# A fourth buffer for streamed weights in a two-block transformer kernel

## The chip, the core and the metric

The kernel is one program on one core of a Trainium2 chip, started once. What is compared is the device time of one execution in microseconds (us); of several executions the median counts. The engines are TensorE (PE; PEld is its weight load, which overlaps the multiplication), VectorE (DVE), ScalarE (ACT), GpSimd (POOL) and SyncE (SP), which here only issues DMAs. They run side by side and wait for each other by semaphores.

## The reference, cut to what matters

256 tokens of width 1024 pass through two different blocks. Each of the two layers of the first block multiplies by `w_in`, mixes in three ways and multiplies by `w_out`:

```
h = x @ w_in[l]                       # 1024 x 6048, split into ten parts
y_hg  = hgrn2(q, f, i)                # chunked gated recurrence, 8 heads
y_mla = mla(cq, ckv, kr)              # attention over latents, 8 heads
y_mem = attention(mem_q, mem @ w_mem_k, mem @ w_mem_v)
x = layernorm(ALPHA * x + concat(y * silu(gates)) @ w_out[l])
```

The second block modulates by `w_ada` (one row of 6144 numbers from `silu(c)`), attends with dilated windows, pools over four trailing windows, and looks up experts:

```
mod  = silu(c) @ w_ada + b_ada                      # 1024 x 6144
q, k, v, u = split(modulated_rmsnorm(x) @ w_in)
x = x + g1 * (concat(dilated_attention(q, k, v), pool(u)) @ w_out)
h2 = modulated_rmsnorm(x)
eid, gate = top 16 of 128 x 128 product keys, 8 heads per token
x = x + g2 * sum_k gate_k * gelu(h2 . expert_u[eid_k]) * expert_v[eid_k]
out = rmsnorm(x)
```

Everything is float32. A product is made of three TensorE products: `a = ah + al`, where `ah` is `a` rounded to the engine's fast 32-bit form, and `ah*bh + ah*bl + al*bh` is accumulated.

## The kernel before, in words

**The stream of weights.** Every large weight comes through one path. `load` (L168) takes a 512 KB tile named `raw` (128 partitions x 1024 numbers) from the pool `wp` and has SP issue the DMA (L170). `split` (L158) lets ACT copy it to `wh` (L162) and DVE subtract to `wl` (L163). `wp` has three buffers of each of the three names. A `raw` buffer is free when its last reader, the subtraction on DVE, is done; a `wh` and a `wl` when the matmuls that read them are (`mm3`, L216 to L218). `feature` uses two such units of 1024 columns for a bank of 256-column products, `token` four for two banks of 512-column products.

**The stream of modulation weights.** `w_ada` goes through the same `raw` buffers (48 loads), but is read by DVE alone, which adds it, scaled by a number for each partition, to `macc` (L892, L894). A generator `ada_parts` yields between the loads; `tick`, which is called after each unit of weights, advances it at every third unit in the layers and at every unit in the second block. There weights and modulation rows so take turns in the ring of three. Larger tiles (`ws`, `wo`, `wq`, constants) have their own buffers, and SP issues them in the same queue.

**Side work.** Attention and recurrence are generators too, resumed by `tick` between two units, so their small instructions stand between the products on every engine. Each engine executes its instructions in the order that the tile scheduler wrote down when the program was built; the scheduler orders by its own estimates of when operands and buffers are ready, so the number of buffers and their sharing reach into the order of every engine.

**Buffers in the order of the program.** `mla_qkv` (L480) writes the normalized latents `cn` in the pool `ml`; the memory queries `mq` (L676) are in the same pool. `xn`, the normalized input of the second block (L724), shares one slot of the pool `xnp` with the keys `kt` of the layers. `yph` and `ypl` (L1015) are the pooled features, in the pool `bp`.

**Warm matmuls.** `warm` (L220) issues matmuls that nobody reads, on a tile of zeros, behind the last real one: 27 at the start, 50 between the blocks (while x is normalized for the second block), 13 before the experts.

**The experts.** POOL issues 256 indirect gathers of 1 MB (L1254); their first needs the experts' indices of the first token tile, which come from a chain through the whole of both blocks. DVE and PE consume the rows (L1320, L1332).

Of the kernel before, what the change touches and what calls it, by code (L numbers as in the profile page):

```python
# [8 lines left out]
F = mybir.dt.float32  # L9
R = mybir.dt.float32r  # L10
# [8 lines left out]
S = 256  # L19
# [12 lines left out]
WARM = (27, 50, 13)  # L32
# [116 lines left out]
class Prog:  # L149
# [16 lines left out]
        return wh, wl  # L166

    def load(self, src, n):  # L168
        raw = self.wp.tile([128, 1024], F, name="raw")
        self.nc.sync.dma_start(raw[:, :n], src)  # L170
        return raw

# [44 lines left out]
        mm(ps, a[0], b[1], start=False, stop=False)  # L217
        self.last_mm = mm(ps, a[1], b[0], start=False, stop=stop)  # L218

    def warm(self, n, ps=None):  # L220

        if ps is None:
            ps = self.pph.tile([128, 512], F, name="bank")
        for _ in range(n):
            m = self.nc.tensor.matmul(ps, self.zero, self.zero[:, None, :].to_broadcast([128, 4, 128]), start=True, stop=True)
            if self.last_mm is not None:
                self.tc.add_manual_dep(m.ins, self.last_mm.ins.name, NOSYNC, reason="fills the time behind it")

# [251 lines left out]
    def mla_qkv(self, l, pm, rows, ws, out):  # L480

        nc = self.nc
        cn = self.ml.tile([128, 2, 416], F, name="cn")
        ss = self.sm.tile([128, 4], F, name="ss")
        sq = self.h2.tile([128, 384], F, name="pt", bufs=2)
        for tt in range(2):
            nc.scalar.activation(sq[:, :256], pm[tt][:, :256], AF.Square, accum_out=ss[:, tt:tt + 1])
            nc.scalar.activation(sq[:, 256:], pm[tt][:, 256:384], AF.Square, accum_out=ss[:, 2 + tt:3 + tt])
        self.rstd(ss[:, 0:2], ss[:, 0:2], 1.0 / 256, self.eps6)
        self.rstd(ss[:, 2:4], ss[:, 2:4], 1.0 / 128, self.eps6)  # L490
        for tt in range(2):
            nc.vector.scalar_tensor_tensor(cn[:, tt, :256], pm[tt][:, :256], ss[:, tt:tt + 1], rows[:, 128:384], op0=OP.mult, op1=OP.mult)
            nc.scalar.activation(cn[:, tt, 384:], pm[tt][:, 384:416], AF.Copy)
            nc.vector.scalar_tensor_tensor(cn[:, tt, 256:384], pm[tt][:, 256:384], ss[:, 2 + tt:3 + tt], rows[:, 384:512], op0=OP.mult, op1=OP.mult)
        return self.mla_rest(ws, cn, out)
# [122 lines left out]
    def layer(self, l, x, xt, mem):  # L618
        nc, I = self.nc, self.I
# [10 lines left out]
        n = 4  # L630
# [45 lines left out]
        mq = self.ml.tile([128, 4, S], F, name="mq")  # L676
        for j in range(2):
            ps = self.feature(W[n], xt)
# [15 lines left out]
        def halves(cg):  # L694
            nonlocal n
            n += 1
            for j, u in enumerate(self.half_units(W[n - 1])):
                yield j, [t.rearrange("p (k c) -> p k c", k=2) for t in u]
# [21 lines left out]
        us = list(halves(1))  # L720
# [7 lines left out]
        for tt in range(2):  # L728
# [8 lines left out]
            for cg in range(2):  # L737
                c = slice(cg * 512, (cg + 1) * 512)
# [7 lines left out]
            if l + 1 == NL:  # L746
                self.normed(x, tt, ss[tt], self.xn[:, tt, :])
        if l + 1 == NL:
            self.warm(WARM[1])
            return None, None  # L750
        xt = self.affine_transposed(x, self.lnc[:, l, 0, :], self.lnc[:, l, 1, :], lambda kg: self.new_xt(), self.h2, "pt")
        mv = self.mem_values(l + 1, nxt[1])
# [220 lines left out]
    def block2(self, x, bp, bk, hp, wq):  # L973

        nc, I = self.nc, self.I
        W, xn = I["wu2"], self.xn
# [6 lines left out]
        wp = bp.tile([128, 512], F, name="wpool")  # L983
# [15 lines left out]
        def tokens(t, j):  # L999
            ps = self.token([W[j], W[j + 1]], ht)  # L1000
            for tt in range(2):
                nc.scalar.activation(t[:, tt, :], ps[tt], AF.Copy)
# [3 lines left out]
        for h in range(8):  # L1006
            for tt in range(2):
                c = slice(128, 384) if tt else slice(0, 128)
# [3 lines left out]
        features(1)  # L1012
        self.start(self.dilated((4, 5), 0, qT, kT, v, y))
        tokens(u, 6)
        yp = [bp.tile([128, 4, S], R, name=n) for n in ("yph", "ypl")]  # L1015
        self.pooling(u, band, wp, yp, bp)
        self.pph.release()
        self.pacc.release()
# [32 lines left out]
        def hidden(tt, ss):  # L1051

            t = bk.tile([128, D], F, name="xn")
            self.normed(x, tt, ss, t)
            yield
            for j in range(2):
                ps = self.pps.tile([128, 4, 128], F, name="bank")
                for k in range(4):
                    f = 4 * j + k
                    nc.tensor.transpose(ps[:, k, :], t[:, f * 128:(f + 1) * 128], self.ident)  # L1060
                for k in range(4):
                    f = 4 * j + k
                    d = self.hidden[:, f, tt * 128:(tt + 1) * 128]
                    scale, shift = self.mod[4][:, f:f + 1], self.mod[3][:, f:f + 1]
                    if k % 2:
                        nc.vector.tensor_scalar(d, ps[:, k, :], scale, shift, op0=OP.mult, op1=OP.add)
                    else:
                        nc.scalar.activation(d, ps[:, k, :], AF.Identity, scale=scale, bias=shift)
                yield
# [20 lines left out]
        for _ in attended(0):  # L1090
            pass
        self.hid = self.big.tile([128, D], F, name="big")
        self.warm(WARM[2], self.hid[:, 0:512])
        for _ in hidden(0, ss[0]):
            pass

# [243 lines left out]
def body(tc, I, O):  # L1340
    nc = tc.nc
    p = Prog(tc, I)
    with tc.tile_pool(name="c0", bufs=1) as c0, tc.tile_pool(name="xp", bufs=1) as xp, tc.tile_pool(name="sm", bufs=4) as sm, \
            tc.tile_pool(name="mo", bufs=1) as mo:
        p.pps, p.pacc, p.pph = [tc.alloc_tile_pool(name=n, bufs=b, space=PSUM) for n, b in (("pps", 2), ("pacc", 4), ("pph", 2))]
        x = xp.tile([128, 2, D], F, name="x")
        wp = tc.alloc_tile_pool(name="wp", bufs=3)
        xnp = tc.alloc_tile_pool(name="xnp", bufs=1)
        p.wp, p.sm, p.xnp, p.gp = wp, sm, xnp, mo
        with tc.tile_pool(name="cp", bufs=1) as cp, tc.tile_pool(name="xtp", bufs=4) as xtp, tc.tile_pool(name="h4", bufs=3) as h4, \  # L1350
                tc.tile_pool(name="h2", bufs=2) as h2, tc.tile_pool(name="ml", bufs=1) as ml:
            p.xtp, p.h4, p.h2, p.ml = xtp, h4, h2, ml
            mt = p.mem_load()
            p.zero = c0.tile([128, 128], R, name="zero")
            nc.vector.memset(p.zero.bitcast(F), 0.0)
            p.warm(WARM[0])
            p.setup(cp, c0)
            p.ada_setup(mo)
            mk, mt = p.mem_keys(0, mt)
            nc.sync.dma_start(x, I["x"])  # L1360
            p.tables(cp, c0)
            xt = p.x_transposed(x)
            mem = [mk, p.mem_values(0, mt)]
            for l in range(NL):
                xt, mem = p.layer(l, x, xt, mem)
        hp = tc.alloc_tile_pool(name="hp", bufs=1, side="right")
        wq = tc.alloc_tile_pool(name="wq", bufs=3, side="right")
        bk = tc.alloc_tile_pool(name="bk", bufs=1, side="right")
        p.mo = hp
        with tc.tile_pool(name="b2", bufs=1) as bp:  # L1370
            rest = p.block2(x, bp, bk, hp, wq)
        xnp.release()
        wp.release()
        p.peer(x, rest, bk, wq, O)
        wq.release()
        hp.release()
        p.big.release()
        p.half.release()
        p.pps.release()
# [16 lines left out]
```

## Time and profile before

| | us |
|---|---|
| median of 3 runs | 1429.11 (1427.68 to 1431.29) |
| the profiled execution | 1429.64 |
| its span, first to last instruction | 1427.8 |
| PE busy | 1265.4 (89%) |
| DVE busy | 990.6 (69%) |
| ACT busy | 582.9 (41%) |
| mean granted TensorE clock | 0.965 |

A granted clock of 1.00 is 2.4 GHz, 0.50 is 1.2 GHz. Stages of the span: constants, memory keys and the input until 36 us; layer 0 to about 325; layer 1 to 605.87; the 50 warm matmuls to 617.37; the second block up to the first gather at 736.77; gathers and experts until 1403.26; the end. Names in the rows are those of the kernel's tiles; `bank` and `half` are PSUM tiles. "L170" is line 170 of the kernel. A DMA's landing is the time from its issue to its completion as the trace shows it. Rows name the releaser of a wait behind an arrow.

### The profile page before, as it was taken

Reading aid. Unit: us, or ns where it says so; the run is one execution under the profiler, and the core shown is the slowest. Engines: PE = TensorE matmul, PEld = TensorE weight load, DVE = VectorE, ACT = ScalarE, POOL = GpSimd, SP = SyncE. Lnnn points to the kernel's source line nnn. Section 1 sums busy time; section 2 is a strip of 40 time slices with the busy share of each in tenths; the row PEclk is TensorE's granted clock in tenths of the full one; section 3 lists DMA queues with packets and bytes.
Section 4 is the critical chain, followed back from the end, with each engine's and each line's share of the span. In section 5 each row is a group of like instructions: output and inputs, shape, how many; then the busy total and the mean of one; then the engine's idle time right before and its main releaser. Section 6 shows DMA issues by size and latency. Waiting matters only on the chain.

```text
span 1427.8 us, 17019 instructions
## 1 busy us (share of the span) xinstructions
PE 1265.4 (89%) x5722; PEld 865.6 (61%) x5722; DVE 990.6 (69%) x2042; ACT 582.9 (41%) x1286; POOL 241.4 (17%) x260
## 2 busy tenths in 40 slices
PE   8999999998999999998979898899777777878765
PEld 7888997776888988877664554454323333333322
DVE  6488889757579887576468565677777777775554
ACT  5566656535467676343335422222223212221112
POOL 0000000000000000000022333334333333333330
PEclk9999999999999999999999999999999998889999
DMA  8464355576462553587439899999999999999993
GB/s 291 146 206 149 115 188 163 178 236 205 167 208 89 163 163 104 177 323 236 141 124 382 327 421 421 420 420 421 421 421 421 420 421 421 421 420 421 422 421 141
DMA packets 73096, 405.29 MB, mean 284 GB/s; under 512 B 8753, under 2 KB 9137, under 8 KB 38065
## 3 DMA queue, kind: packets, MB, share of 16 engines
q0 software_dynamic: 36864, 268.45, 45.6%
q1 hardware_dynamic: 36144, 135.75, 28.8%
q8 instruction: 46, 0.75, 0.2%
q14 instruction: 42, 0.34, 0.1%
HBM read 403.12 MB, written 1.05 MB: 283 GB/s over the span
## 4 chain that ended last, share of the span: by engine, by line
PE 45%; DMA 36%; DVE 10%; ACT 5%; issue 3%; POOL 0%; DVEq 0%; POOLq 0%; ACTq 0%; SPq 0%
DMA uv<-in_puv_dram,eid 29%; PE half L1332 9%; PE bank L217 7%; PE bank L218 7%; PE bank L216 7%; DMA raw<-in_wu_dram 6%; PE bank L1216 2%; DVE wl L163 2%; PE bank L375 2%; ACT wh L162 2%; DVE uv L1320 2%; PE bank L465 1%; PE half L1086 1%; PE bank L514 1%; DMA raw<-in_wada_dram 1%
## 5 line engine op out<-in xcount | busy, mean ns | idle before, releaser
L1332 PE MATMUL half<-uv,d 128*128 128x512 f32 x1024 | 487.0, 630 | 105.8 <-ACT d L1330 105.5
L1254 POOL DMA_INDIRECT uv<-in_puv_dram,eid x256 | 241.2, 942 | 1150.9 <-DVE tv L1141 737.1
L1332 PEld LDWEIGHTS half<-uv,d 128*128 128x128 f32 x1024 | 200.8, 201 | 374.5 <-issue 228.4
L1320 DVE CUSTOM_DVE_ANT_0 uv<-big,uv 128x1024 f32<-128x1024 f32 x256 | 312.6, 1222 | 161.8 <-DMA uv<-in_puv_dram,eid 156.7
L163 DVE TENSOR_TENSOR wl<-raw,wh 128x1024 fp32r<-128x1024 f32 (+1 forms) x164 | 198.9, 1213 | 113.6 <-ACT wh L162 112.3
L162 ACT ACTIVATE wh<-raw 128x1024 fp32r<-128x1024 f32 (+1 forms) x164 | 171.8, 1050 | 176.9 <-DMA raw<-in_wu_dram 86.8
L217 PE MATMUL bank<-wl,xh 128*128 128x512 f32 (+1 forms) x384 | 153.6, 400 | 2.2 <-DVE wl L163 2.2
L1325 ACT ACTIVATE dot<-dot 128x4 f32<-128x4 f32 (+2 forms) x70 | 14.3, 204 | 343.7 <-DVE dot L1320 343.6
L216 PE MATMUL bank<-wh,xh 128*128 128x512 f32 (+1 forms) x384 | 154.5, 404 | 0.0
L218 PE MATMUL bank<-wh,xl 128*128 128x512 f32 (+1 forms) x384 | 153.1, 399 | 0.0
L218 PE MATMUL bank<-xh,wl 128*128 128x256 f32 x384 | 112.9, 294 | 7.1 <-DVE wl L163 7.1
L216 PE MATMUL bank<-xh,wh 128*128 128x256 f32 x384 | 112.7, 294 | 4.4 <-ACT wh L162 4.4
L217 PE MATMUL bank<-xl,wh 128*128 128x256 f32 x384 | 110.0, 287 | 0.0
L1330 ACT ACTIVATE d<-ident,dot 128x128 f32<-128x128 f32 x256 | 82.8, 390 | 29.5 <-DVE dot L1326 27.4
L217 PEld LDWEIGHTS bank<-wl,xh 128*128 128x128 f32 x384 | 72.7, 189 | 16.9 <-DVE wl L163 3.6
L216 PEld LDWEIGHTS bank<-wh,xh 128*128 128x128 f32 x384 | 72.7, 189 | 14.4 <-ACT t L338 0.5
L218 PEld LDWEIGHTS bank<-wh,xl 128*128 128x128 f32 x384 | 72.7, 189 | 14.3
L218 PEld LDWEIGHTS bank<-xh,wl 128*128 128x128 f32 x384 | 73.7, 192 | 9.3 <-DVE wl L163 8.7
L216 PEld LDWEIGHTS bank<-xh,wh 128*128 128x128 f32 x384 | 74.0, 193 | 8.0 <-ACT wh L162 5.4
L217 PEld LDWEIGHTS bank<-xl,wh 128*128 128x128 f32 x384 | 73.6, 192 | 0.4
L894 DVE SCALAR_TENSOR_TENSOR macc<-raw,sc,macc 128x1024 f32<-128x1024 f32 x42 | 53.7, 1278 | 10.5 <-DMA raw<-in_wada_dram 10.5
L1216 PEld LDWEIGHTS bank<-hidden,wq 128*128 128x128 f32 x352 | 52.9, 191 | 11.5 <-issue 7.4
(295 smaller groups left out, 1642.5 us busy)
## 6 DMA issues: line engine op xcount, KB each, us to landing
raw<-in_wu_dram SPq DMA_DIRECT2D x156, 512.0 KB, 4.3
raw<-in_wada_dram SPq DMA_DIRECT2D x48, 512.0 KB, 4.2
wq<-in_wu_dram SPq DMA_DIRECT2D x8, 1024.0 KB, 9.3
uv<-in_puv_dram,eid POOLq DMA_INDIRECT x256
raw<-in_wm_dram SPq DMA_DIRECT2D x8, 416.0 KB, 3.9
ws<-in_ws_dram SPq DMA_DIRECT2D x2, 1536.0 KB, 9.4
raw<-in_memT_dram SPq DMA_DIRECT2D x4, 512.0 KB, 4.6
lnr<-in_rows_dram SPq DMA_DIRECT2D x2, 1024.0 KB, 6.1
```

The costliest lines, as they stand in the source:

```text
L162: nc.scalar.activation(wh[:, :n], raw[:, :n], AF.Copy)
L163: self.last_split = nc.vector.tensor_tensor(wl[:, :n], raw[:, :n], wh[:, :n].bitcast(F), op=OP.subtract)
L216: mm(ps, a[0], b[0], start=start, stop=False)
L217: mm(ps, a[0], b[1], start=False, stop=False)
L218: self.last_mm = mm(ps, a[1], b[0], start=False, stop=stop)
L375: nc.tensor.matmul(ps[:, h, k, :], st[:, c:c + 128], mv[:, c:c + 128], start=True, stop=True)
L894: self.behind(nc.vector.scalar_tensor_tensor(acc, raw, self.sc[:, k:k + 1], acc, op0=OP.mult, op1=OP.add))
L1216: mm = nc.tensor.matmul(ps[:, m, :n], w[:, c:c + 128], ht[:, k, c0:c0 + n], start=k == 0, stop=k == 7)
L1254: nc.gpsimd.indirect_dma_start(out=t, out_offset=None, in_=I["puv"], in_offset=bass.IndirectOffsetOnAxis(ap=eid[:, u, k:k + 1], axis=0))
L1320: self.last_split = nc.vector.tensor_tensor_reduce(out=uv[:, 0:D], in0=hid, in1=uv[:, 0:D], scale=1.0, scalar=0.0, op0=OP.mult, op1=OP.add ...
L1330: nc.scalar.activation(d, self.ident, AF.Copy, scale=dot[:, u, k:k + 1])
L1332: self.last_v = nc.tensor.matmul(acc[cg], d, uv[:, D + cg * 512:D + (cg + 1) * 512], start=u % 8 == 0 and k == 0, stop=u % 8 == 7 and k == 15)
```

## The change

`load` asks for four `raw` buffers where it had three; `wh` and `wl` stay at three. 4 KB in each partition are found for it in four ways. The tile of zeros goes: the warm matmuls at the start read a zeroed `wh` buffer, the 50 between the blocks the `wh` of the last unit of layer 1 (that buffer is then not free until they are done), and the 13 later ones the pooled features. `cn` shares its slot with `mq`. The two halves of the pooled features become one tile that takes the slot of `xn`. The number of transfers and of matmuls is the same.

```
--- before.py
+++ after.py
@@ -166,7 +166,7 @@
         return wh, wl
 
     def load(self, src, n):
-        raw = self.wp.tile([128, 1024], F, name="raw")
+        raw = self.wp.tile([128, 1024], F, name="raw", bufs=4)
         self.nc.sync.dma_start(raw[:, :n], src)
         return raw
 
@@ -217,12 +217,12 @@
         mm(ps, a[0], b[1], start=False, stop=False)
         self.last_mm = mm(ps, a[1], b[0], start=False, stop=stop)
 
-    def warm(self, n, ps=None):
+    def warm(self, n, w, ps=None):
 
         if ps is None:
             ps = self.pph.tile([128, 512], F, name="bank")
         for _ in range(n):
-            m = self.nc.tensor.matmul(ps, self.zero, self.zero[:, None, :].to_broadcast([128, 4, 128]), start=True, stop=True)
+            m = self.nc.tensor.matmul(ps, w[:, 0:128], w[:, None, 0:128].to_broadcast([128, 4, 128]), start=True, stop=True)
             if self.last_mm is not None:
                 self.tc.add_manual_dep(m.ins, self.last_mm.ins.name, NOSYNC, reason="fills the time behind it")
 
@@ -480,7 +480,7 @@
     def mla_qkv(self, l, pm, rows, ws, out):
 
         nc = self.nc
-        cn = self.ml.tile([128, 2, 416], F, name="cn")
+        cn = self.ml.tile([128, 2, 416], F, name="cn", tag="mq")
         ss = self.sm.tile([128, 4], F, name="ss")
         sq = self.h2.tile([128, 384], F, name="pt", bufs=2)
         for tt in range(2):
@@ -746,7 +746,7 @@
             if l + 1 == NL:
                 self.normed(x, tt, ss[tt], self.xn[:, tt, :])
         if l + 1 == NL:
-            self.warm(WARM[1])
+            self.warm(WARM[1], us[-1][1][0].rearrange("p k c -> p (k c)"))
             return None, None
         xt = self.affine_transposed(x, self.lnc[:, l, 0, :], self.lnc[:, l, 1, :], lambda kg: self.new_xt(), self.h2, "pt")
         mv = self.mem_values(l + 1, nxt[1])
@@ -1012,7 +1012,8 @@
         features(1)
         self.start(self.dilated((4, 5), 0, qT, kT, v, y))
         tokens(u, 6)
-        yp = [bp.tile([128, 4, S], R, name=n) for n in ("yph", "ypl")]
+        yp = self.xnp.tile([128, 2, 4, S], R, name="yp", tag="xn")
+        yp = [yp[:, 0], yp[:, 1]]
         self.pooling(u, band, wp, yp, bp)
         self.pph.release()
         self.pacc.release()
@@ -1090,7 +1091,7 @@
         for _ in attended(0):
             pass
         self.hid = self.big.tile([128, D], F, name="big")
-        self.warm(WARM[2], self.hid[:, 0:512])
+        self.warm(WARM[2], yp[0].rearrange("p k t -> p (k t)"), self.hid[:, 0:512])
         for _ in hidden(0, ss[0]):
             pass
 
@@ -1351,9 +1352,9 @@
                 tc.tile_pool(name="h2", bufs=2) as h2, tc.tile_pool(name="ml", bufs=1) as ml:
             p.xtp, p.h4, p.h2, p.ml = xtp, h4, h2, ml
             mt = p.mem_load()
-            p.zero = c0.tile([128, 128], R, name="zero")
-            nc.vector.memset(p.zero.bitcast(F), 0.0)
-            p.warm(WARM[0])
+            zero = wp.tile([128, 1024], R, name="wh")
+            nc.vector.memset(zero[:, 0:128].bitcast(F), 0.0)
+            p.warm(WARM[0], zero)
             p.setup(cp, c0)
             p.ada_setup(mo)
             mk, mt = p.mem_keys(0, mt)
```

The scheduler writes another order in several places. SP, in the second block, from the load of the unit before the alibi tables (raw_6198) to that of raw_6240: `wo` and `wq` are tiles of the output and query weights, 1 MB each, `wada` rows are modulation weights, `wu2` rows units of weights. Before:

```order
L170 DMA raw_6198<-in_wu2_dram 128x1024
L1074 DMA wo1_6048<-in_wu2_dram 128x2048
L170 DMA raw_6216<-in_wada_dram 128x1024
L170 DMA raw_6219<-in_wu2_dram 128x1024
L1078 DMA wq_6730<-in_wu2_dram 128x2048
L1078 DMA wq_6732<-in_wu2_dram 128x2048
L170 DMA raw_6237<-in_wada_dram 128x1024
L170 DMA raw_6240<-in_wu2_dram 128x1024
```

The same part after the change:

```order
L170 DMA raw_6198<-in_wu2_dram 128x1024
L170 DMA raw_6216<-in_wada_dram 128x1024
L1075 DMA wo1_6048<-in_wu2_dram 128x2048
L1079 DMA wq_6729<-in_wu2_dram 128x2048
L170 DMA raw_6219<-in_wu2_dram 128x1024
L170 DMA raw_6237<-in_wada_dram 128x1024
L1079 DMA wq_6731<-in_wu2_dram 128x2048
L170 DMA raw_6240<-in_wu2_dram 128x1024
```

The modulation row raw_6216 and `wo1` change places, one `wq` comes ahead of raw_6219 instead of behind it, and the other moves behind the modulation row raw_6237, directly ahead of raw_6240.

ACT, at the end of the 50 warm matmuls: wh_6115 is the first half of the second unit of the second block, xn_5854 the normalized input, nt the modulated one on its way to the transposed operand.

```order
 L288 ACTIVATE nss_5856<-nss_5856,eps_136 128x1
 L290 ACTIVATE nss_5856<-nss_5856 128x1
+L940 ACTIVATE xn_5854<-x_76,nss_5856 128x512
 L162 ACTIVATE wh_6115<-raw_6113 128x1024
-L940 ACTIVATE xn_5854<-x_76,nss_5856 128x512
 L781 ACTIVATE nt_5994<-bank_5993,mcol_196 128x256
 L781 ACTIVATE nt_6004<-bank_6003,mcol_196 128x256
```

The copy into wh_6115, which takes the buffer whose matmuls end last, moves behind the second half of the normalization.

DVE, right behind it: nl0 is the low part of the operand that the first products of the second block read, macc_6050 the sum of the modulation rows.

```order
 L779 TENSOR_SCALAR nt_5994<-bank_5993,mcol_196 128x256
 L779 TENSOR_SCALAR nt_6004<-bank_6003,mcol_196 128x256
+L894 SCALAR_TENSOR_TENSOR macc_6050<-raw_6119,sc_190,macc_6050 128x1024
 L263 TENSOR_TENSOR nl0_5992<-nt_5994,nh0_5991 128x512
 L263 TENSOR_TENSOR nl0_5992<-nt_6004,nh0_5991 128x512
-L894 SCALAR_TENSOR_TENSOR macc_6050<-raw_6119,sc_190,macc_6050 128x1024
 L779 TENSOR_SCALAR nt_6016<-bank_6015,mcol_196 128x256
 L779 TENSOR_SCALAR nt_6026<-bank_6025,mcol_196 128x256
```

A modulation step (raw_6119) moves ahead of the two subtractions that make nl0.

## Rows read from the trace of the kernel before

**Rows 1.** The page, chain that ended last: its lines with the largest shares

```profile
DMA uv<-in_puv_dram,eid 29%; PE half L1332 9%; PE bank L217 7%; PE bank L218 7%; PE bank L216 7%; DMA raw<-in_wu_dram 6%; PE bank L1216 2%; DVE wl L163 2%; PE bank L375 2%; ACT wh L162 2%; DVE uv L1320 2%; PE bank L465 1%; PE half L1086 1%; PE bank L514 1%; DMA raw<-in_wada_dram 1%
```

**Rows 2.** Windows; columns: length, busy us (instructions) by engine, PEclk, DMA share, GB/s

```profile
0.00:36.00 36.00, 31.56 (x172) 27.48 (x173) 23.91 (x53) 19.84 (x26) 0.20 (x4) 0.95 0.82 290
...
281.58:325.30 43.72, 38.94 (x207) 32.19 (x205) 27.05 (x29) 16.81 (x19) 0.00 (x0) 1.00 0.70 220
340.00:360.00 20.00, 15.17 (x93) 13.83 (x92) 13.65 (x20) 8.18 (x24) 0.00 (x0) 1.00 0.65 231
360.00:605.87 245.87, 243.53 (x1545) 209.58 (x1544) 185.11 (x306) 150.31 (x315) 0.00 (x0) 1.00 0.47 151
...
736.77:1403.26 666.49, 547.05 (x1412) 258.57 (x1411) 454.67 (x1155) 171.78 (x446) 241.23 (x256) 0.94 1.00 412
```

**Rows 3.** Windows, the ring in block 2 and the wait before it, same columns

```profile
630.50:644.87 14.37, 10.97 (x54) 8.84 (x53) 9.53 (x21) 1.74 (x3) 0.00 (x0) 0.88 0.91 327
...
644.87:679.00 34.13, 31.34 (x179) 27.12 (x180) 21.56 (x28) 12.86 (x22) 0.00 (x0) 0.90 0.73 233
```

**Rows 4.** Chain of waits, 640 to 662: start us, length us, what

```profile
637.55 7.15 DMA raw<-in_wu_dram
...
647.12 4.12 DMA raw<-in_wada_dram
...
651.33 1.30 DVE macc L894
...
652.64 5.15 DMA raw<-in_wu_dram
...
657.87 1.06 ACT wh L162
...
658.96 1.23 DVE wl L163
...
660.21 5.02 DMA raw<-in_wada_dram
```

**Rows 5.** Landing of raw loads, 572 to 600

```profile
DMA to landing us min/median/max: 3.1/3.6/3.7
```

**Rows 6.** Tile raw, 644.87 to 679: loads with duration ns, first and last start; landings

```profile
L170 SPq DMA_DIRECT2D raw<-in_wu_dram x8: 327/328/328, 644.9 to 675.0; - x8
...
L170 SPq DMA_DIRECT2D raw<-in_wada_dram x8: 327/327/328, 647.1 to 677.2; - x8
...
DMA to landing us min/median/max: 3.6/4.5/5.1
```

**Rows 7.** Landing of raw loads, 281.58 to 325.30

```profile
DMA to landing us min/median/max: 3.4/4.2/6.2
```

**Rows 8.** PE's waits, 640 to 705: us in total, times, longest

```profile
PE bank L216 <- ACT wh L162: 3.8, 3, 2.6
```

**Rows 9.** PE's waits, 270 to 360, same columns

```profile
PE bank L216 <- ACT wh L162: 4.4, 4, 2.9
```

**Rows 10.** SP's issues around 631: start us, us, engine, line, operation, names

```profile
631.29 0.90 SPq L1078 DMA_DIRECT2D wq<-in_wu_dram  x2
```

**Rows 11.** Start of the second block: start us, us, engine, line, operation, idle before

```profile
605.87 11.50 PE L225 MATMUL bank<-zero 128*128 128x512 f32 x50
...
614.59 1.04 ACT L162 ACTIVATE wh<-raw 128x1024 fp32r<-128x1024 f32 x1
...
617.45 1.22 DVE L163 TENSOR_TENSOR wl<-raw,wh 128x1024 fp32r<-128x1024 f32 x1
...
620.04 1.29 DVE L263 TENSOR_TENSOR nl<-nt,nh 128x512 fp32r<-128x512 f32 x2 [0.24 <-ACT nh L262]
...
620.07 0.50 PE L216 MATMUL bank<-nh,wh 128*128 128x256 f32 x2
```

**Rows 12.** Last reads of cn: duration ns, first and last start us

```profile
L520 PE MATMUL bank<-ident,cn x4: 269/270/272, 62.1 to 368.6; 128*32 128x128 f32 x4
```

**Rows 13.** First writes of mq, same columns

```profile
L680 ACT ACTIVATE mq<-bank x4: 569/580/582, 194.1 to 506.1; 128x512 f32<-128x512 f32 x4
```

More of the change, by code (lines that the diff above doesn't have):

```diff
@@ L168, in load @@
     def load(self, src, n):
-        raw = self.wp.tile([128, 1024], F, name="raw")
+        raw = self.wp.tile([128, 1024], F, name="raw", bufs=4)
         self.nc.sync.dma_start(raw[:, :n], src)
@@ L218, in mm3, with warm @@
         self.last_mm = mm(ps, a[1], b[0], start=False, stop=stop)
-    def warm(self, n, ps=None):
+    def warm(self, n, w, ps=None):
         if ps is None:
@@ L224, in warm @@
         for _ in range(n):
-            m = self.nc.tensor.matmul(ps, self.zero, self.zero[:, None, :].to_broadcast([128, 4, 128]), start=True, stop=True)
+            m = self.nc.tensor.matmul(ps, w[:, 0:128], w[:, None, 0:128].to_broadcast([128, 4, 128]), start=True, stop=True)
             if self.last_mm is not None:
@@ L482, in mla_qkv @@
         nc = self.nc
-        cn = self.ml.tile([128, 2, 416], F, name="cn")
+        cn = self.ml.tile([128, 2, 416], F, name="cn", tag="mq")
         ss = self.sm.tile([128, 4], F, name="ss")
@@ L748, in layer @@
         if l + 1 == NL:
-            self.warm(WARM[1])
+            self.warm(WARM[1], us[-1][1][0].rearrange("p k c -> p (k c)"))
             return None, None
@@ L1014, in block2 @@
         tokens(u, 6)
-        yp = [bp.tile([128, 4, S], R, name=n) for n in ("yph", "ypl")]
+        yp = self.xnp.tile([128, 2, 4, S], R, name="yp", tag="xn")
+        yp = [yp[:, 0], yp[:, 1]]
         self.pooling(u, band, wp, yp, bp)
@@ L1092, in block2 @@
         self.hid = self.big.tile([128, D], F, name="big")
-        self.warm(WARM[2], self.hid[:, 0:512])
+        self.warm(WARM[2], yp[0].rearrange("p k t -> p (k t)"), self.hid[:, 0:512])
         for _ in hidden(0, ss[0]):
@@ L1353, in body @@
             mt = p.mem_load()
-            p.zero = c0.tile([128, 128], R, name="zero")
-            nc.vector.memset(p.zero.bitcast(F), 0.0)
-            p.warm(WARM[0])
+            zero = wp.tile([128, 1024], R, name="wh")
+            nc.vector.memset(zero[:, 0:128].bitcast(F), 0.0)
+            p.warm(WARM[0], zero)
             p.setup(cp, c0)
```

## Prediction, made before the changed kernel was run

> **What bounds the kernel now.** I read the chain that ended last first: its largest piece is the gathers, 29% [rows 1]. The windows show why: from 736.77 to 1403.26 the DMA engines are busy all the time (share 1.00, 412 GB/s) [rows 2]. Nothing in that stage changes, so it stays 666.5 us long, and what can change is the moment at which it begins. Everything that is gained or lost on the way to the first gather therefore passes to the end one to one.
>
> On that way TensorE is the bound nearly everywhere: in layer 1 it is busy for 243.53 of 245.87 us [rows 2]. A fourth weight buffer has nothing to give there, because loads already arrive before they are wanted. It has something to give only where PE stands still for a load. The windows show three such places: the end of layer 0, 281.58 to 325.30, with PE busy for 38.94 of 43.72; the start of layer 1, 340 to 360, with 15.17 of 20.00 [rows 2]; and the second block, 630.50 to 679, with 10.97 of 14.37 and 31.34 of 34.13 [rows 3]. PE's waits in these stretches begin at L216, for the copy `wh`: 3.8 us in three waits in the second block, 4.4 us in four around the end of layer 0 [rows 8, 9]. The copy itself takes 1.06 us [rows 4]; what is late is the load ahead of it.
>
> The chain of waits in the second block is a ring that feeds itself [rows 4]: a modulation load issued at 647.12 lands after 4.12, DVE adds it in 1.30, at 652.64 SP issues the next weight load into the same buffer, it lands after 5.15, ACT copies in 1.06, DVE subtracts in 1.23, and at 660.21 the buffer is filled again. Each load is issued when DVE gives a buffer back, not when SP or PE wants it. That is the signature of too few buffers, and the reader should look for it in the starts: 644.9 and 647.1 for the first loads of the two kinds, 675.0 and 677.2 for the last, eight of each [rows 6].
>
> **The change part by part.** The sum is made against the profiled execution, 1429.64 (span 1427.8 and 1.8 around it); that is 0.5 above the median of 1429.11, and I take the 0.5 off at the end.
>
> *The ring in the second block, 644.87 to 679.* Sixteen loads in 34.13 us are 2.13 each; with three buffers a buffer turns in 6.4 us (one turn in the chain is 5.52 for a modulation load, 7.57 for a weight load, mean 6.5 [rows 4]). Four buffers with the same turn would give 1.60 per load, 25.6 us. Two floors lie near. The DMA engines were busy for 0.73 of the stretch, 24.9 us. PE was busy for 31.34; the mean granted clock of 0.90 (stretches at 1.2 GHz among those at 2.4) cost about 3.4 of it, so its work is 27.9 at full clock [rows 3]. The gain so has an end at 34.1 − 27.9 = 6.2. The other end is none, if a load takes as much longer as there are more of them in flight. How much longer is the unknown. Where PE sets the pace a load lands in 3.6 [rows 5], in the full ring in 4.5 [rows 6], so keeping the ring full cost 0.9; I take as much again for the fourth, since that is the nearest pair of rows. The turn is then 7.3, a load 1.83, the stretch 29.2: **−4.9** (0 to −6.2).
>
> *The load before it.* The last wait ahead of the ring, 2.6 us [rows 8], ends with the load issued at 637.55 that took 7.15 to land [rows 4], beside the two 1 MB loads `wq` issued at 631.29 [rows 10]. With a fourth buffer it is issued about one turn earlier. But the DMA engines were busy for 0.91 of 630.50 to 644.87 [rows 3], so the same bytes can end earlier by only 9% of 14.37: **−1.3** (0 to −2.6). The order of SP spreads the `wq` loads but moves no more bytes.
>
> *The operand of the 50 warm matmuls.* They run from 605.87 for 11.50 us, to 617.37 [rows 11]. They now hold one of three `wh` buffers, and the copy that was made at 614.59 must go into it. It starts at about 617.4 and ends 1.04 later, its subtraction (before: 617.45, 1.22 long) starts at 618.4 and ends at 619.6, 1.0 later than before. Queued behind it on DVE is the affine step, and then the subtraction that makes nl (620.04), without which the first products (620.07) can't go on [rows 11]. So **+1.0**. The modulation step that now stands ahead of nl would add up to 1.3 [rows 4], and a wait of PE may drop the clock: in 630.50 to 644.87 a mean clock of 0.88 cost 1.7 us [rows 3]. The ends are 0, if the affine step was waited for anyway, and +4.0.
>
> *The end of layer 0 and the start of layer 1.* PE stands still for 4.8 us in each [rows 2]. In the first the loads (one modulation row to about three weights) keep DMA busy for 0.70, so there is room; but part of PE's waits is for DVE and for `wh` and `wl` buffers, which stay three. I take half: **−2.4** (0 to −4.8). In the second the 1.5 MB tile `ws` comes in the same queue among the weights, and it still does: two fifths, **−2.0** (0 to −4.8).
>
> *The beginning, 0 to 36.* PE idles 4.4 us, DMA is busy for 0.82 [rows 2]. One weight load more goes ahead of x. It could let PE start sooner, or make x later by one load, 1.56 us (24.9 over 16): **0** (−3 to +1.6).
>
> *The sharing.* `cn` is read last at 62.1 in layer 0 and 368.6 in layer 1, `mq` is first written at 194.1 and last at 506.1 [rows 12, 13], so no wait arises: more than 100 us of other work covers it in either layer. If that cover were gone, the price would be the wait of one copy, 0.58 us [rows 13]. The pooled features come into `xn`'s slot long after the first products of the second block have read it, and cost nothing for the same reason. The warm matmuls read other data at the same size: 0.
>
> The sum is −4.9 − 1.3 + 1.0 − 2.4 − 2.0 = −9.6, so 1420.0, and against the median **1419.5**.
>
> A rule speaks against the change. The Trainium skill, "DMA: Bandwidth & Descriptors", section "Latency and other measured facts", gives an HBM access 0.2 us on average and 2 us at high load. As an estimate from that page, a landing could grow by 1.8, the turn to 8.2 and a load to 2.05, and the ring would give back only 1.3 of its 4.9. The trace so far shows half of such a growth, 3.6 to 4.5, with the third buffer [rows 5, 6]; whether the fourth adds the rest no run here shows yet.
>
> **The rivals.** *Loads that only take longer.* The longest landing of the end of layer 0 is 6.2 [rows 7], 1.7 over the ring's median. If that becomes the rule, the turn is 8.1, a load 2.03, and the ring gives 1.6; the other places in proportion (a third) about 0.4, 0.8 and 0.7; with the +1.0 the sum is −2.5: 1426.6. For it speaks the share of 0.91 beside the `wq` loads, against it the 0.73 and 0.70 elsewhere. The same time comes out if DVE or the three `wh` buffers end the waits instead.
>
> *PE becomes the bound everywhere.* Then the ring gives 6.2, the load before it 2.6 and the 1.7 of lost clock behind it, the ends of layers 4.8 each, less 1.0: −19.1, 1410.0. For it speaks that PE never waits where loads run ahead; against it that PE's waits are also for side work.
>
> *Slower.* The warm matmuls' buffer costs its whole +4.0, the modulation step and a clock drop among it, and the ring gives nothing: 1433.1. It decides from a landing of 6.6 in the ring (turn 8.5, over four 2.13 as before). For it speaks the order of DVE, in which the modulation step stands directly ahead of nl; against it that a landing of 6.6 is above every one in the ring so far, at most 5.1 [rows 6].
>
> **How the numbers follow.** The forecast (1415 to 1424) 0.47; loads that take longer (1424 to 1429.5) 0.27; PE the bound (1404 to 1415) 0.15; slower (1429.5 to 1436) 0.11. About 0.3%, 4.3 us, is what a measurement of this kernel can tell from no change. Below 1424.8 lie the first, the third and a sixth of the second: faster 0.67. Above 1433.4 lies most of the slower case and some mishap I haven't named: 0.10. Between: 0.23. For 8 in 10 the range goes from 1409 to 1430: it leaves out half of the PE case and most of the slower one.
>
> **What would show it.** In the new profile the ring's sixteen loads take 28 to 31 us instead of 34.1, landings there have a median near 5.4, and PE waits at L216 for less than 2 us in 640 to 705. PE is busy for over 93% of the end of layer 0. The first product of the second block comes 1 us later after the warm matmuls' end than before (2.7). The first gather starts near 727, and the gathers take 666 us as before. I am wrong on the ring if landings pass 6, on the warm operand if the first product is not late or is late by over 2, and on the whole if the gathers' stage changes its length.

## The result, and the profile after

The changed kernel takes **1407.12 us** (median of 4 runs, 1405.14 to 1408.56); the kernel before, on the same chip, 1428.73 (4 runs, 1427.68 to 1431.29). The ratio is 0.984, 95% interval 0.9825 to 0.9855. The prediction, 1419.5 with 1409 to 1430, had the sign right and the size wrong by more than half: 9.6 us were forecast and 21.6 came. The profiled span went from 1427.8 to 1404.8, by 23.0.

To see where, I take the same piece of work in both traces: the start of the n-th product of line L216, of which each kernel has 880. The table has the time from one mark to the next in us, for the two kernels and for the experiments that follow.

| mark (stage up to it) | before | changed | e1 three | e5 wh 4 | e2 layers | e3 block 2 | e9 pause, 3 | e7 ahead | e12 later | e11 43 warm |
|---|---|---|---|---|---|---|---|---|---|---|
| 209th (start, half of layer 0) | 164.0 | 163.5 | 163.9 | 167.1 | 162.2 | 165.9 | 164.0 | 162.2 | 161.2 | 162.1 |
| 353rd (rest, output product begun) | 117.9 | 114.6 | 118.1 | 117.7 | 114.6 | 116.3 | 113.9 | 114.6 | 114.5 | 114.6 |
| 481st (end of layer 0, start of layer 1) | 98.7 | 87.0 | 100.5 | 98.5 | 87.0 | 98.5 | 87.5 | 87.7 | 87.4 | 87.8 |
| 753rd (layer 1) | 214.0 | 212.1 | 214.1 | 215.0 | 215.5 | 213.4 | 229.9 | 212.2 | 213.1 | 212.5 |
| 801st (warm matmuls, first four units) | 39.3 | 41.8 | 42.8 | 43.1 | 43.0 | 42.7 | 39.2 | 40.8 | 38.8 | 39.7 |
| 865th (ring of block 2) | 62.7 | 55.8 | 62.5 | 62.2 | 62.7 | 56.0 | 62.4 | 55.6 | 57.6 | 55.6 |
| first gather | 40.1 | 39.7 | 39.7 | 39.7 | 39.6 | 39.7 | 39.7 | 39.7 | 41.2 | 39.7 |
| end of span | 691.0 | 690.4 | 693.2 | 692.7 | 690.0 | 692.5 | 690.4 | 691.1 | 692.3 | 691.0 |

The first row is not sharp: the changed kernel, run again in a later set, had 160.6 there. Half of the gain (11.7 us) lies at the end of layer 0 and the start of layer 1, 6.9 in the ring of the second block, 3.4 and 2.0 in the rest of the layers, and 2.5 are lost behind the warm matmuls. The windows of the changed kernel, with the columns of [rows 2]:

```profile
278.06:365.09 87.03, 84.55 (x480) 71.86 (x478) 57.13 (x74) 45.59 (x74) 0.00 (x0) 1.00 0.65 216
577.15:618.92 41.77, 38.75 (x211) 33.23 (x210) 30.82 (x52) 18.37 (x34) 0.00 (x0) 0.96 0.76 278
...
629.18:658.53 29.35, 28.98 (x182) 24.97 (x182) 21.55 (x29) 12.88 (x22) 0.00 (x0) 1.00 0.83 271
674.75:714.48 39.73, 37.32 (x202) 28.49 (x201) 15.15 (x48) 8.88 (x19) 0.00 (x0) 1.00 0.06 18
714.48:1380.40 665.92, 552.73 (x1412) 261.07 (x1412) 454.43 (x1155) 171.85 (x446) 242.50 (x256) 0.93 1.00 412
```

The first answers to this window of the kernel before, in which the same 128 products took 98.70 us; the second row is a part of it that the prediction had left out:

```profile
281.96:380.66 98.70, 88.00 (x480) 73.41 (x478) 58.71 (x75) 46.41 (x75) 0.00 (x0) 0.98 0.60 193
325.20:337.70 12.50, 11.31 (x48) 9.00 (x49) 8.40 (x13) 8.95 (x15) 0.00 (x0) 0.86 0.69 209
```

PE now works for 84.55 of 87.03 there, at the full clock. The ring's sixteen loads, 629.18 to 658.53, take 29.35 us instead of 34.13 [rows 3], and PE is busy for all but 0.4 of it, with the clock at 1.00 instead of 0.90. The stage of the gathers is 665.9 long, as before [rows 2], and starts at 714.48 instead of 736.77, so the 22.3 us that were gained ahead of it did pass to the end. The landings in the ring, as in [rows 6]:

```profile
L170 SPq DMA_DIRECT2D raw<-in_wu_dram x8: 327/328/328, 629.2 to 654.7; - x8
L170 SPq DMA_DIRECT2D raw<-in_wada_dram x8: 327/328/328, 630.4 to 655.9; - x8
...
DMA to landing us min/median/max: 4.6/5.2/5.5
```

The median went from 4.5 to 5.2, and a load now goes every 1.83 us (29.35 over 16).

What PE waited for in the stretch that gained most, in the kernel before (282 to 381, beside the 4.4 us of [rows 9]; columns: us in total, times, longest):

```profile
PE bank L218 <- DVE wl L163: 3.0, 4, 0.8
PE bank L777 <- ACT x L741: 1.8, 1, 1.8
PE bank L217 <- DVE wl L163: 1.4, 2, 0.8
```

And in the changed kernel (278 to 365), all that is left:

```profile
PE bank L503 <- DVE cn L494: 0.8, 1, 0.8
PE bank L217 <- DVE xl L587: 0.6, 1, 0.6
PE bank L217 <- DVE wl L163: 0.6, 1, 0.6
PE bank L218 <- DVE wl L163: 0.4, 1, 0.4
```

10.6 us of waits became 2.4. The clock cost about 1.7 more, all of it between 325.20 and 337.70 (0.86 over 12.50 us). The 8.2 and the 1.7 are 9.9 of the 11.7. The waits for `wl` went with those for `wh`, though neither got a buffer. The chain of waits of the kernel before shows how the two hang together (284 to 300; start us, us, what):

```profile
285.40 6.24 DMA raw<-in_wu_dram
...
291.75 1.07 ACT wh L162
...
292.83 1.24 DVE wl L163
...
294.12 0.39 PE bank L218
```

PE's wait at L218 is put down to DVE, but DVE had waited for ACT, and ACT for a load that took 6.24 us to land. Followed back in this way, 6.3 of the 10.6 us end at a load: three of the four waits for `wh` and three of the six for `wl`. The rest have other last releasers. At 284.0 and 285.4 (1.2 us) the copy stood behind other work of ACT that had waited for PE, at 344.0 (0.7) DVE was still busy. The other two are the wait of 0.76 at 317.56 and the one for the layer norm (L777, for x of L741). ACT works in order, and in both a copy ahead of what PE needs had itself waited for PE (L218), that is, for a `wh` buffer. Before:

```profile
315.18 1.06 ACT L162 ACTIVATE wh<-raw 128x1024 fp32r<-128x1024 f32 x1 [2.44 <-PE bank L218]
...
317.56 0.50 PE L217 MATMUL bank<-wl,xh 128*128 128x512 f32 x1 [0.76 <-DVE wl L163]
...
324.58 1.06 ACT L162 ACTIVATE wh<-raw 128x1024 fp32r<-128x1024 f32 x1 [1.70 <-PE bank L218]
...
325.54 1.51 ACT L741 ACTIVATE x<-x,bag 128x512 f32<-128x512 f32 x2
...
326.39 0.44 PE L777 MATMUL bank<-ident,x 128*128 128x128 f32 x2 [1.81 <-ACT x L741]
```

In the changed kernel neither is left, and at L777 the products of the next loads fill PE until x comes:

```profile
313.89 1.52 ACT L741 ACTIVATE x<-x,bag 128x512 f32<-128x512 f32 x2
...
314.76 0.44 PE L777 MATMUL bank<-ident,x 128*128 128x128 f32 x2
```

Last, the start of the second block, to be held against [rows 11]:

```profile
588.32 11.53 PE L225 MATMUL bank<-wh 128*128 128x512 f32 x50
...
599.88 1.06 ACT L162 ACTIVATE wh<-raw 128x1024 fp32r<-128x1024 f32 x1 [1.98 <-PE bank L225]
...
603.02 1.28 DVE L894 SCALAR_TENSOR_TENSOR macc<-raw,sc,macc 128x1024 f32<-128x1024 f32 x1
604.22 1.29 DVE L263 TENSOR_TENSOR nl<-nt,nh 128x512 fp32r<-128x512 f32 x2
604.95 0.38 PE L217 MATMUL bank<-nl,wh 128*128 128x256 f32 x1 [1.08 <-DVE nl L263]
```

The copy did wait for the warm matmuls (1.98), the modulation step did go ahead of nl, and nl starts 4.4 us after their end (599.85) instead of 2.7 (617.37 to 620.04 before). The clock then fell as well: 0.96 over the 41.77 us of that window is 1.7 lost.

The rest of the layers, from the 209th to the 353rd product and from the 481st to the 753rd, in the kernel before:

```profile
164.04:281.96 117.92, 115.97 (x746) 100.58 (x744) 94.17 (x153) 70.98 (x161) 0.00 (x0) 0.99 0.55 172
380.66:594.67 214.01, 211.66 (x1376) 183.86 (x1375) 169.47 (x282) 135.73 (x295) 0.00 (x0) 1.00 0.49 155
```

And in the changed one:

```profile
163.50:278.06 114.56, 113.78 (x746) 99.21 (x744) 95.03 (x155) 72.37 (x161) 0.00 (x0) 1.00 0.57 180
365.09:577.15 212.06, 211.00 (x1376) 183.74 (x1375) 169.50 (x282) 134.97 (x295) 0.00 (x0) 1.00 0.49 157
```

PE's idle time fell by 1.2 us in the first and by 1.3 in the second. In the first the clock was at 0.50 once, from 180.0 to 183.4, which cost 1.7.

### The profile page after: what moved, and what is told of

It reads as the page before. It is cut to its first block, busy times and chain, and to the rows that moved or that the text cites. A ratio compares the mean times of both kernels' runs of the same rounds, so it can differ in the third digit from the quotient of the medians.

```text
span 1404.8 us, 17024 instructions
## 1 busy us (share of the span) xinstructions
PE 1262.4 (90%) x5722; PEld 864.4 (62%) x5722; DVE 988.1 (70%) x2042; ACT 583.1 (42%) x1286; POOL 242.7 (17%) x260
## 4 chain that ended last, share of the span: by engine, by line
PE 57%; DMA 28%; DVE 8%; ACT 4%; issue 2%; POOL 0%; DVEq 0%; ACTq 0%; POOLq 0%
DMA uv<-in_puv_dram,eid 26%; PE half L1333 11%; PE bank L217 9%; PE bank L218 9%; PE bank L216 9%; PE bank L375 3%; PE bank L1217 3%; DMA raw<-in_wu_dram 2%; DVE uv L1321 2%; PE bank L465 2%; DVE wl L163 1%; PE half L1087 1%; PE bank L514 1%; PE bank L441 1%; ACT wh L162 1%
## 5 line engine op out<-in xcount | busy, mean ns | idle before, releaser
L1333 PE MATMUL half<-uv,d 128*128 128x512 f32 x1024 | 492.6, 636 | 99.7 <-ACT d L1331 99.6
L216 PE MATMUL bank<-wh,xh 128*128 128x512 f32 (+1 forms) x384 | 154.0, 403 | 0.0
L217 PE MATMUL bank<-wl,xh 128*128 128x512 f32 (+1 forms) x384 | 152.4, 397 | 0.6 <-DVE wl L163 0.6
L218 PE MATMUL bank<-wh,xl 128*128 128x512 f32 (+1 forms) x384 | 152.4, 397 | 0.0
L218 PE MATMUL bank<-xh,wl 128*128 128x256 f32 x384 | 112.3, 292 | 2.7 <-DVE wl L163 2.7
L216 PE MATMUL bank<-xh,wh 128*128 128x256 f32 x384 | 111.7, 291 | 0.8 <-ACT wh L162 0.8
L217 PE MATMUL bank<-xl,wh 128*128 128x256 f32 x384 | 110.4, 288 | 0.6 <-DVE xl L587 0.6
L217 PEld LDWEIGHTS bank<-wl,xh 128*128 128x128 f32 x384 | 72.5, 189 | 14.5 <-DVE wl L163 1.5
L218 PEld LDWEIGHTS bank<-wh,xl 128*128 128x128 f32 x384 | 72.4, 188 | 13.9
L216 PEld LDWEIGHTS bank<-wh,xh 128*128 128x128 f32 x384 | 72.4, 189 | 13.6 <-ACT t L338 0.5
L218 PEld LDWEIGHTS bank<-xh,wl 128*128 128x128 f32 x384 | 73.9, 192 | 4.1 <-DVE wl L163 3.3
L216 PEld LDWEIGHTS bank<-xh,wh 128*128 128x128 f32 x384 | 74.1, 193 | 2.7 <-ACT wh L162 1.3
L217 PEld LDWEIGHTS bank<-xl,wh 128*128 128x128 f32 x384 | 73.7, 192 | 1.7 <-DVE xl L587 0.8
L1217 PE MATMUL bank<-hidden,wq 128*128 128x128 f32 (+1 forms) x352 | 59.5, 323 | 0.1
```

The source lines that it names most:

```text
L216: mm(ps, a[0], b[0], start=start, stop=False)
L1217: mm = nc.tensor.matmul(ps[:, m, :n], w[:, c:c + 128], ht[:, k, c0:c0 + n], start=k == 0, stop=k == 7)
L1333: self.last_v = nc.tensor.matmul(acc[cg], d, uv[:, D + cg * 512:D + (cg + 1) * 512], start=u % 8 == 0 and k == 0, stop=u % 8 == 7 and k == 15)
```

## The experiments

The kernel before ran in each set of kernels on the same chip (1430.27, 1429.42 and 1429.22 in the three sets); ratios are to it, and a difference in us that stands with a ratio is worked out from the ratio.

**e1_three: everything but the fourth buffer.**

```
-        raw = self.wp.tile([128, 1024], F, name="raw", bufs=4)
+        raw = self.wp.tile([128, 1024], F, name="raw", bufs=3)
```

> All edits of the change but the fourth buffer: raw stays at three. Theory (the fourth buffer alone gives the time, the sharing gives nothing and the warm operand costs a little): 1428.7 as before plus 1 to 2.6 for the warm operand, 1429 to 1432, with the half-clock stretches and the waits for loads at 284 to 300 and 340 to 360 back. Rival (sharing slots lets the scheduler write a better order): 1413 to 1422.

1434.8 us (1425.47 to 1439.76, 10 runs), ratio 1.0028 (1.0007 to 1.0049), 4.0 us slower. The sharing, and the order that the scheduler writes with it and three buffers, are no source of the gain; without the buffer they cost. The table has 1.8 more at the end of layer 0 and 3.5 more behind the warm matmuls, a little more than expected. The order that the scheduler writes with four buffers comes only together with the fourth buffer, so no run separates these two.

**e5_wh4: the same room for a fourth wh.**

```
-        wh = self.wp.tile([128, 1024], R, name="wh")
+        wh = self.wp.tile([128, 1024], R, name="wh", bufs=4)      # and raw with bufs=3
```

> The room of the fourth raw buffer goes to a fourth wh buffer: raw three, wh four, wl three. Theory (only the landing of raw loads was waited for): 1430 to 1435, as with three of each. Rival (half of the waits around the end of layer 0 were for wh buffers, as the prediction took them): 1425 or less.

1434.99 (1427.3 to 1439.62, 10 runs), 1.0028 (1.001 to 1.0047): the same as with three of each. The stage at the end of layer 0 is 2.0 shorter than in e1, 1.7 of it by the clock; PE's idle time there is 10.4 us, beside 11.2 in e1 and 2.5 in the changed kernel. It is the `raw` buffer that matters; the rival, on which the prediction's halves rested, is out for `wh`. A fourth `wl` was not run.

**e2_layers and e3_block2: the fourth buffer in one half only.**

```
 e2: at the end of layer 1
+            self.held = self.wp.tile([128, 1024], R, name="raw", bufs=4)
+            nc.vector.memset(self.held[:, 0:128].bitcast(F), 0.0)
...
-        self.warm(WARM[2], yp[0]..., self.hid[:, 0:512])
+        self.warm(WARM[2], self.held, self.hid[:, 0:512])
 e3: at the start
-            zero = wp.tile([128, 1024], R, name="wh")
+            zero = p.held = wp.tile([128, 1024], R, name="raw", bufs=4)
...
+            self.warm(1, self.held, ps)
+            self.warm(WARM[1] - 1, us[-1][1][0]..., ps)
```

> Four raw buffers in the two layers; from the end of layer 1 one of them is held by a tile that nobody fills, until the last warm matmuls read it, so the second block has three. Theory (the layers give 17 us, the second block 7 less 2.6): 1428.7 - 17.4 + 2.6 = about 1414, first gather near 721. Rival (the second block gives most, as predicted 6.2 of 9.6, and the early start of the layers is given back there): 1419 to 1424.

> Three raw buffers in the two layers, because a tile that nobody fills holds the fourth until one of the 50 warm matmuls reads it; four in the second block. Theory: the layers end as before (605.9), the second block gives 6.9 and costs 2.6: 1424 to 1425. Rival (second block gives most): 1416 to 1420.

e2: 1414.73 (4 runs), 0.9888 (0.986 to 0.9917), 16.0 below the kernel before. e3: 1426.34 (10 runs), 0.997 (0.9955 to 0.9985), 4.3 below. Against e1, which has the same sharing, they are 20 and 8.3 below. The table splits cleanly: in e2 the stage at the end of layer 0 takes 87.0 and the ring 62.7, in e3 98.5 and 56.0. The layers give over two thirds of the gain, where the prediction had put less than half.

**e9_pause3: three buffers, but fewer loads at the end of layer 0.** The kernel before, with the modulation rows moved out of that stretch.

```
+        if l == 0:
+            self.every = 10 ** 9              # ahead of the output product
...
+        else:
+            self.every = 2                    # layer 1, behind its first pair
```

> The kernel before, with its three buffers, but no modulation rows are loaded in the output product of layer 0 and the beginning of layer 1; those loads follow in layer 1, every second unit instead of every third. Theory (all of PE's waits at the end of layer 0 and the start of layer 1 come from the ring of raw loads): the stretch between them loses 8 to 11 of the 11.7 us that the fourth buffer took there, 1418 to 1422. Rival (half of the waits are for DVE and for wh and wl buffers): 4 us, 1425 to 1426.

1430.28 (10 runs), 1.0008 (0.9988 to 1.0029): no change in all, so both expected times were missed, but the stage in question did nearly what the theory said. It takes 87.46 us instead of 98.70, with three buffers of each kind:

```profile
277.87:365.33 87.46, 83.38 (x463) 70.27 (x462) 49.80 (x67) 46.17 (x75) 0.00 (x0) 1.00 0.51 170
365.33:595.26 229.93, 222.40 (x1409) 193.04 (x1408) 182.98 (x297) 135.92 (x295) 0.00 (x0) 0.97 0.51 170
```

Of the 11.2 us, about 1.7 are work of PE that moved with the rows (16 products `bank<-ones,macc`, 366.8 to 368.5 in the kernel before), so the fewer loads gave some 9.5 of the 11.7. PE's idle time fell from 10.7 to 4.1. DVE had 8.9 us less to do in the stretch, but the changed kernel, in which DVE does as much as before (57.13 us, before 58.71), lost the waits as well. So most of these waits go when the ring of `raw` loads has room, also with three `wh` and three `wl`, and so do those that did not end at a load by the rows, the two behind a `wh` buffer among them. By what way those go is not shown. The second row tells what was not expected: layer 1 took 229.9 instead of 214.0. What the two stages ahead of it had gained, 4.0 and 11.2, came back there: PE was idle for 7.5 us instead of 2.3, and the clock of 0.97 cost 6.8.

**e6_us0 and e7_ahead: another operand for the 50 warm matmuls.**

```
-            self.warm(WARM[1], us[-1][1][0].rearrange("p k c -> p (k c)"))
+            self.warm(WARM[1], us[0][1][0].rearrange("p k c -> p (k c)"))     # e6
+            self.warm(WARM[1], self.ahead[0])                                # e7
```

> The change with one edit: the 50 warm matmuls read the wh of the last unit but one of layer 1 instead of the last. Theory (the copy made behind them waits because they hold the buffer it goes into): the copy no longer waits for PE L225, the subtraction that makes nl starts less than 3.5 us after the warm matmuls' end (4.5 in the changed kernel, 2.7 before), 1404.5 to 1406. Rival (it is the modulation step ahead of nl on DVE, or this buffer is the one the copy needs then): no change, 1407.

e6: 1408.51 (4 runs), 0.9847 (0.9816 to 0.9878). As a test it failed: with another operand, the scheduler gave the copy that operand's buffer, and it waited as before:

```profile
597.65 1.06 ACT L162 ACTIVATE wh<-raw 128x1024 fp32r<-128x1024 f32 x1 [2.00 <-PE bank L225]
```

> The change with one edit: the 50 warm matmuls read the wh of the first unit of the second block, which is already there and is kept for the products behind them anyway. Theory (the copy into the second unit's wh waited for the warm matmuls because their operand held the only buffer it could have): the copy comes before they end, the first L217 product starts 3.5 us after their end (5.2 in the changed kernel, 3.4 before), and the time is 2 to 3.5 below the changed kernel's. Rival (the modulation step ahead of nl on DVE makes it late): first L217 product still about 4.5 to 5.2 behind, no change in time.

e7: 1406.37 (1405.55 to 1408.91), 0.984 (0.9822 to 0.9857), beside 1406.55 and 0.9834 (0.9818 to 0.9851) for the changed kernel in the same set (e8_after):

> The changed kernel again, on the chip of this set, so that the others can be held against it: 0.984 of the kernel before.

In e7 the copy is made nearly 10 us before the warm matmuls end, and the first L217 product starts 4.4 us behind their end (599.38), not 5.1:

```profile
587.85 11.53 PE L225 MATMUL bank<-wh 128*128 128x512 f32 x50
588.47 1.06 ACT L162 ACTIVATE wh<-raw 128x1024 fp32r<-128x1024 f32 x1 [0.33 <-DMA raw<-in_wu_dram]
...
600.56 1.28 DVE L894 SCALAR_TENSOR_TENSOR macc<-raw,sc,macc 128x1024 f32<-128x1024 f32 x1
...
602.99 1.29 DVE L263 TENSOR_TENSOR nl<-nt,nh 128x512 fp32r<-128x512 f32 x2 [0.25 <-ACT nh L262]
603.74 0.58 PE L217 MATMUL bank<-nl,wh 128*128 128x256 f32 x1
```

Both theories hold a part: the buffer held 0.7 us, and the modulation step still stands ahead of nl. In time no gain can be told.

**e12_later, e11_warm43, e13_both: the rest of that delay.** On e7, the modulation rows at every second unit in the first four units (e12), 43 warm matmuls for 50 (e11), or both (e13).

```
+        self.every = 2                 # e12: ahead of features(0), and 1 behind it
-WARM = (27, 50, 13)
+WARM = (27, 43, 13)                    # e11
```

> The kernel whose warm matmuls read the first unit's wh, with the modulation rows at every second unit instead of every one in the first four units of the second block. Theory (what is left of the late start there is the modulation step that DVE does ahead of nl): the first L217 product comes 3 to 3.5 us after the warm matmuls' end (4.4 in that kernel), 1 to 2.5 us less in all if no clock drop follows, 1404 to 1405.5. Rival (two modulation loads more stand at the end of the block, where the ring is the bound): the gain is given back before the output product, no change, 1406.4.

> The kernel whose warm matmuls read the first unit's wh, with 43 of them instead of 50 (1.6 us fewer). Theory (the transposes behind them wait for the warm matmuls, since xn is ready 1.3 us before their end): 1 to 1.5 us less. Rival (the chain through nt and nl on ACT and DVE sets the first product, and PE only stands still earlier): no change, or 1.7 more where the clock drops once more.

> Both edits of this set at once. Theory: their gains add, 2 to 4 us below the kernel with neither, 1402.5 to 1404.5. Rival: one chain bounds both, no more than the better of the two.

e12: 1409.55 (1406.96 to 1411.67), 0.9872 (0.9844 to 0.9901). The first L217 product starts 3.4 us behind the warm matmuls, as in the kernel before, and the stage up to the 801st product takes 38.8 us, at the full clock, instead of 41.8: that is the whole of the delay, 0.7 us of it by the buffer (e7) and 1.0 by the modulation step. Of the 2.0 between e7's 40.8 and this stage, 1.7 are the clock. But the two loads that were put off stand at the end of the block now, where PE waits for them again: the ring's stage takes 57.6 instead of 55.6, and the one to the gathers 41.2 instead of 39.7.

```profile
576.29:615.08 38.79, 37.47 (x212) 31.79 (x211) 28.67 (x50) 18.15 (x34) 0.00 (x0) 1.00 0.73 269
615.08:672.68 57.60, 51.37 (x270) 42.16 (x268) 40.10 (x54) 24.23 (x44) 0.00 (x0) 0.94 0.79 268
```

e11: 1404.52 (1400.85 to 1405.23), 0.9827 (0.9799 to 0.9854), the lowest median of all, and 1.0 less in the stage than e7; its interval holds the changed kernel's 0.984, so it isn't shown to be faster than that, only than the kernel before. e13: 1408.39 (1403.36 to 1409.6), 0.985 (0.9819 to 0.988): the gains don't add, the end of the block takes them back as in e12, and more: the ring's stage takes 61.4 there, with the clock at 0.89, and the one to the gathers 41.2.

## Why the prediction was wrong

- **What bounds the kernel: right.** The gathers' stage kept its length, and a gain ahead of it came through.
- **The ring in the second block and the load before it: right, the exact size in part by luck.** −4.9 was forecast for the sixteen loads and −4.8 came (34.13 to 29.35), with the forecast 1.83 per load. The landings grew by 0.7, to 5.2, where I had put 0.9 from the nearest pair of rows. But PE was busy for 28.98 of the 29.35 us at the full clock and waited for next to nothing, so its own work, which the prediction had put at 27.9, would have held the stretch near 29 with shorter landings too. That the two bounds lie so close is luck. The two steps together were −6.2; the table and e3 have −6.9 and −6.7. The load before the ring has no stretch of its own, so its −1.3 was not measured alone. The Trainium skill ("DMA: Bandwidth & Descriptors", "Latency and other measured facts") gives an HBM access 0.2 us on average and 2 us at high load. The estimate from it put the whole growth of 1.8 on the fourth buffer, and by it the ring would have given 1.3; the trace shows 0.7 of growth there. From 3.6, where a load went every 2.8 us, to 5.2 the landings grew by 1.6 in all. The 3.6 and the 4.5 of [rows 5, 6] are both from the kernel with three buffers, at two paces, and not from before and after a third one.
- **The warm matmuls' operand: the mechanism right, the size low.** +1.0 was forecast, about +2.5 came, within the ends 0 and +4.0. I had the modulation step ahead of nl and the clock only in the end of the range; both happened. e7 puts 0.7 us of the first product's delay to the buffer, and e12 shows the rest gone when the modulation step is moved.
- **The end of layer 0 and the start of layer 1: this step failed.** It said "part of PE's waits is for DVE and for `wh` and `wl` buffers, which stay three. I take half", and two fifths for the second window: −4.4. It measured −11.7. e5 shows that a `wh` buffer in place of the `raw` one gives nothing in all, and e9 that with fewer loads in the ring three buffers of each kind lose little there (4.1 us idle instead of 10.7). Half of the waits at L217 and L218 for DVE's `wl` (2.3 of 4.4 us) were the same late loads, seen one engine further on; I had read the last releaser and not followed it back. The others went too, though by the rows they do not end at a load; how stays open. The ends failed too: the two windows stopped at 325.3 and began at 340, and what lies between was in no term: 1.1 of the 1.8 us of wait for the layer norm, and the clock of 0.86, which cost 1.7.
- **The rest of the layers: nothing forecast, −3.4 and −2.0 measured.** "Loads already arrive before they are wanted" was read from layer 1's mean, 243.53 of 245.87 busy, and the prediction shows no window of layer 0 between 36 and 281 for it. The 3.4 stand in each kernel with four buffers in the layers (114.5 to 114.6 for that stage, 116.3 to 118.1 with three and the rows in their old place). 1.2 of the 3.4 and 1.3 of the 2.0 are idle time of PE. 1.7 of the 3.4 are the clock, which fell in the kernel before after a wait of 0.75 at L218 and did not fall after the same wait in e9; that part isn't shown to be the buffer's doing.
- **The sharing at nothing: nearly.** In the changed kernel and in e1 no writer of `cn`, `mq`, `xn` or the pooled features waits for a reader of the slot that it shares, but the order that the scheduler wrote with it and three buffers is 4.0 us slower (e1).

The rival "PE becomes the bound everywhere" came nearest, at 1410.0, with a chance of 0.15 that was too low. It left out 325 to 340 and the rest of the layers as well: it had 9.6 for the layers, where the last three stages of the table up to the 753rd product have 17.1. It stood only 3 us high because it had 10.5 for the second block's ring and the load before it, where 6.9 came; that is luck. The range ended at 1409 because it was drawn through this rival.

## What to carry to other kernels

Follow a wait back to its root before dividing it: where the same loads pass through two engines in turn, PE's waits for either of them can have one cause. Here a buffer ahead of the first took most of them (10.6 us to 2.4). A wait that is removed can take with it what stood queued behind the late instruction and the clock that fell after it, so windows for a bound must join without gaps. And what is freed in one place of a full ring can be asked for in another: e9 and e12 moved the same bytes and got nothing.

## What the hardware showed that was not expected

The landing of a 512 KB load took 3.6 us where one went every 2.8 us [rows 5], 4.5 in the ring of three (one every 2.13) and 5.2 in the ring of four (one every 1.83), while the bytes per second of the ring rose from 233 to 271 GB/s. Landing over interval, as an estimate of the loads in flight, gives 1.3, 2.1 and 2.8, so that one more in flight cost about 1 us of landing at each step. The granted clock fell to 0.50 in other places from kernel to kernel: in six stretches ahead of the gathers in the kernel before and in three in the changed one, none of them between 30 and 600 us there, though single waits of PE of up to 0.8 us stayed. A wait of 0.75 us at L218, near 180 us, was followed by such a fall in the kernel before and by none in e9:

```profile
180.00 0.58 PE L218 MATMUL bank<-xh,wl 128*128 128x256 f32 x1 [0.75 <-DVE wl L163]
```

The same in e9, with the window of the 209th to the 353rd product there:

```profile
179.97 0.39 PE L218 MATMUL bank<-xh,wl 128*128 128x256 f32 x1 [0.75 <-DVE wl L163]
163.99:277.87 113.88, 112.47 (x729) 97.43 (x728) 89.89 (x147) 71.45 (x161) 0.00 (x0) 1.00 0.50 164
```
